# Where the rows of the next block are kept while they wait to be normalised

## The chip, the cores and the metric

The kernel runs on one core of a Trainium2 chip. The metric is the device time of one execution in microseconds (us). The kernel before took 2994.34 us as the median of three runs.

## What is computed

One step of a one-layer encoder, for a prompt of 2048 rows and a sample of 64 rows, all in float32. Cut to what matters here:

```python
mod = jax.nn.silu(c) @ p['w_ada'] + p['b_ada']
sh1, sc1, gt1, sh2, sc2, gt2 = [m[:, None, :] for m in jnp.split(mod, 6, axis=-1)]
h = rms_norm(x, p['norm1_g']) * (1 + sc1) + sh1
z = h @ p['w_in']
glu_a, glu_b, q, k, v, g_conv, g_attn = jnp.split(z, offs, axis=-1)
u = glu_a * jax.nn.sigmoid(glu_b)
# conv module on u; band attention (the own chunk and 8 before it) on the normalised q, k and v
merged = jax.nn.sigmoid(g_conv) * conv_out + jax.nn.sigmoid(g_attn) * attn_out
x = x + gt1 * (merged @ p['w_o'])
# then a second norm with sh2 and sc2, a SwiGLU, and the residual with gt2
```

The modulation `mod` is needed in two parts. The first norm needs `sh1` and `sc1`; the other four vectors (`gt1`, `sh2`, `sc2`, `gt2`) are needed much later.

## The kernel before

A product of two float32 matrices is made of three products of parts (`mm3`): each operand is split into a high part and a low part (`whi` and `wlo`, `hh` and `hl`), so TensorE does three matmuls where one would stand.

The first phase, some 1200 us, goes through the rows in four blocks (`PBLOCKS`): the sample's 64 rows with 512 of the prompt, then three blocks of 512. Within a block the stages come in the order of `ORDER`: the q projection, the first GLU column group (stage 0), k, group 1, v, groups 2 and 3, and the gates `g`. Attention of a block, its convolution and its k/q norms run beside these products as generators in lanes; a planner (`Stream`) decides by estimated engine loads when each lane makes its next step, and what was registered with `stream.at` happens when its planned time comes. The framework's own scheduler then sets the order of the instructions on each engine and allots the buffers of each tag, so a change of what waits for which buffer can move instructions of all engines.

While a block's gates are computed, the rows of the next block are prepared. Each of the four row tiles (128 rows of 1024) goes through `norm_tile`: the row is loaded (`load_x`, a tile called `x_t`), ScalarE squares it (`junk`), VectorE and GpSimd make the inverse root (`ssq`, `t`, then `r` by a power on GpSimd), VectorE scales the row, TensorE turns it in two halves (`pt`), VectorE applies `A1` and `B1` (`h`), ScalarE and VectorE split the result into `hh` and `hl`. The lane `norm_lane` holds two of these generators at a time. The loads are driven by `load_ahead`, which takes the next row from `to_load`: three calls are made at gate `NORM_G` (the eleventh), and one more each time a row's second half has been turned. The rows' buffers have the tag `x`, of which there are three, so the fourth row's load waits until the first row has been turned. The same tag holds `vst` of `store_v` and, in the first block, some of the `kn` tiles of `qk_rows`.

The class `Slabs` (the object `M`) brings the slabs of `w_ada` for the modulation, 512 KB each, into four buffers with the tag `wmod`, in the order of `mod_order`: 16 slabs for `sh1` and `sc1`, used in the first block (keys of five parts), then 32 for the other four vectors, four to each of eight steps (keys of another length). A step is made at the end of each of the GLU stages 0 to 3 of blocks two and three (`MODS`). A slab's load is issued as soon as one of the four buffers is free, whoever will use it and when. So four of the later slabs are loaded in the first block, as the last of the first 16 slabs are used up, and lie in their buffers until the first step of block two; after block three the buffers are not used again.

Weights come through `Weights` (`W`), with five split slabs held; for blocks two to four they are read back as parts that were stored in memory (`w_din_h`, `w_din_l`, `w_dqkv_h`, `w_dqkv_l`). Nearly all loads and stores are issued on SyncE's queue (SP) in one order.

The helper that records every instruction is line 102, so nearly all instructions have that line and are told apart by their tiles; the profile shortens some names (`q2` is `q`, `h32` is `h`).

Of the kernel before, what the change touches and what calls it, by code (L numbers as in the profile page):

```python
# [16 lines left out]
P = 128  # L17
# [15 lines left out]
QB = 512  # L33

PBLOCKS = [(0, 576), (576, 1088), (1088, 1600), (1600, 2112)]
# [11 lines left out]
X_LAG = 8000.0  # L47
# [17 lines left out]
def token_tiles(lo, hi):  # L65
    head = [(0, SMP)] if lo == 0 else []
    return head + [(t, P) for t in range(max(lo, SMP), hi, P)]
# [162 lines left out]
class Slabs:  # L230
# [3 lines left out]
    def __init__(self, sync, other, pool, stream, keys, source, held):  # L234
        self.sync, self.other, self.pool, self.stream = sync, other, pool, stream
        self.keys, self.source, self.held = keys, source, held
        self.ready, self.used, self.given, self.freed = [], 0, 0, 0

    def fill(self):
        while len(self.ready) < min(len(self.keys), self.freed + self.held):  # L240
            (src,), a, b = self.source(self.keys[len(self.ready)])
            w = self.pool.tile([P, a, b], F32, tag="wmod", name="wmod", bufs=self.held)
            i = len(self.ready)
            (self.other if i < self.held and i % 2 else self.sync).dma_start(w, src)
            self.ready.append(w)

    def get(self, key):
        assert self.keys[self.used] == key
        self.used += 1
        while len(self.ready) < self.used:  # L250
            self.free(self.freed + 1)
        return self.ready[self.used - 1]

    def done(self):
        self.given += 1
        self.stream.at(self.stream.when("pe"), lambda n=self.given: self.free(n), True)
# [321 lines left out]
def mod_order():  # L578
    for ct in range(0, KT, 2):
        yield from (("mod", c6, ct // 2, h, 0) for c6 in (0, 1) for h in range(2))  # L580
    yield from (("mod", *half, i) for half in MOD_HALVES for i in range(4))
# [30 lines left out]
def streaming_layer(ctx: ExitStack, tc: tile.TileContext, I, O):  # L612
    nc = tc.nc
    stream = Stream()
    pe, dve, act, gps = (
        Meter(e, n, stream) for e, n in ((nc.tensor, "pe"), (nc.vector, "dve"), (nc.scalar, "act"), (nc.gpsimd, "pool"))
    )
# [10 lines left out]
    def rows(prompt, sample, t, n):  # L628
        return prompt[t - SMP : t - SMP + n] if t >= SMP else sample[t : t + n]
# [129 lines left out]
    def temp(name, shape=(P, 512)):  # L759
        return wk.tile(list(shape), F32, tag="t", name=name, bufs=NT)  # L760
# [353 lines left out]
    def load_x(t, n, pool, tag, bufs, queue=nc.sync):  # L1114
        x_t = pool.tile([P, D], F32, tag=tag, name="x_t", bufs=bufs)
        queue.dma_start(x_t[:n], rows(x_p, x_s, t, n))
        return x_t

    def square(x_t, n):
        ssq = wk.tile([P, 2], F32, tag="ssq", name="ssq", bufs=3)  # L1120
        for j in range(2):
            act.activation(temp("junk")[:n], x_t[:n, 512 * j : 512 * j + 512], AF.Square, accum_out=ssq[:n, j : j + 1])
        stream.after("dve", "act")
        dve.tensor_tensor(ssq[:n, 0:1], ssq[:n, 0:1], ssq[:n, 1:2], ALU.add)
        return rsqrt_mean(wk, ssq[:n, 0:1], n, 1, D)

    ahead_x, to_load = {}, []

    def load_ahead():

        if to_load:
            t = to_load.pop(0)
            ahead_x[t] = load_x(t, P, wa, "x", 3), stream.load["pe"] + X_LAG

    def norm_tile(lo, t, free):

        c = slice(t - lo, t - lo + P)
        while t not in ahead_x:
            load_ahead()
        x_t, landed = ahead_x.pop(t)  # L1140
        yield landed
        r = square(x_t, P)
        yield stream.when("pool")
        dve.tensor_scalar(x_t, x_t, r, None, ALU.mult)
        yield stream.when("dve") + PE_LAG
        for g in range(2):
            pt = ps_g.tile([P, 4, P], F32, tag="gp", name="pt")
            h = temp("h32", (P, 4, P))
            for k in range(4):
                pe.transpose(pt[:, k], x_t[:, (4 * g + k) * P : (4 * g + k + 1) * P], ident)  # L1150
            if g:
                stream.at(stream.when("pe"), load_ahead, True)
            stream.after("dve", "pe")
            for k in range(4):
                kk = 4 * g + k
                dve.tensor_scalar(h[:, k], pt[:, k], A1[:, kk, 0:1], B1[:, kk, 0:1], ALU.mult, ALU.add)
            yield stream.when("dve")
            yield lambda: free["columns"] >= c.stop
            f = slice(4 * g, 4 * g + 4)
            act.activation(hh[:, f, c], h, AF.Copy)  # L1160
            yield stream.when("act")
            dve.tensor_tensor(hl[:, f, c], h, hh[:, f, c].bitcast(F32), ALU.subtract)
    def qkv(b, m, norms):
        lo, hi = PBLOCKS[b]
        tiles = token_tiles(lo, hi)
        ws = {}

        def product(t, n, ps, k):
            if k // 2 not in ws:
                ws[k // 2] = W.get(("qkv", m, k // 2))  # L1170
            wh, wl = ws[k // 2]
            c = slice(t - lo, t - lo + n)
            mm3(ps[:n], hh[:, k, c], hl[:, k, c], wh[:, k % 2], wl[:, k % 2], k == 0, k == KT - 1)
            if (t, n) == tiles[-1] and k % 2:
                W.done()

        for t, n in tiles:
            if t in norms:
                norm_lane.drain([norms[t]])
            ps = ps_g.tile([P, 512], F32, tag="gp", name="ps")  # L1180
            for k in range(KT):
                product(t, n, ps, k)
            if m == 0:
                work.start(qk_rows(ps, n, gqk[:, 0:1], q_d, t, None))
            elif m == 1:
                work.start(qk_rows(ps, n, gqk[:, 1:2], k_d, kcol(t), state_row(ks_p, kn_s, t, n), b == 0 and t > 2 * P))
            else:
                v_rows(ps, n, t)
# [391 lines left out]
    wa = side.enter_context(tc.tile_pool(name="wa", bufs=1, side="right"))  # L1580
    vectors_ = load_vectors()
    first_vectors = next(vectors_)
    M = Slabs(nc.sync, nc.scalar, wa, stream, list(mod_order()), source, 4)
# [8 lines left out]
    for b, stage in ORDER:  # L1592
        lo, hi = PBLOCKS[b]
        if stage == "q":
            free, ahead = {"columns": 0}, {}
            if b + 1 < len(PBLOCKS):
                ahead = {t: norm_tile(hi, t, free) for t, _ in token_tiles(*PBLOCKS[b + 1])}
        if stage == "q" and b == 0:
            pass
        elif stage in ("q", "k", "v"):  # L1600
            qkv(b, "qkv".index(stage), norms)
            if stage == "k":
                work.wide = 3
            if stage == "v":

                def heads(b=b):
                    work.drain()
                    stream.flush()
                    attention(b)
                    if b == 3:  # L1610
                        attn.burst, attn.spacing = 2, 0.0

                stream.at(stream.load["pe"] + HEADS_NS, heads)
        elif stage == "g":
            for g in gates(b, free):
                if g == NORM_G:
                    to_load += list(ahead)
                    for _ in range(3):
                        load_ahead()
                    for gen in ahead.values():  # L1620
                        norm_lane.add(gen)
                if g == SIDE_G and b == len(PBLOCKS) - 1:
                    work.drain()
                    conv.drain()
                    stream.flush()
                    side.close()
                    wc = ctx.enter_context(tc.tile_pool(name="wc", bufs=1, side="right"))
                    cs = tile_chunks(*CBLOCKS[0])[0]
                    src = load_mixed(*cs, 0)
                    first_gates = gate_columns(*cs, 0)  # L1630
            norms = ahead
        else:
            if b == 0 and stage == 1:
                bias_rows()
            if stage == 0:
                conv.drain()
                tail.drain()
                y = wk.tile([P, 4, YW], F32, tag="y", name="y")
            conv.add(convolve(glu(b, stage), y, stage, b))
            if stage == 3:  # L1640
                if b == 0:
                    tail.add(conv_norm(y, 0, SMP, 0))
                    tail.add(conv_norm(y, SMP + HIST, QB, SMP))
                else:
                    tail.add(conv_norm(y, 0, QB, lo))
        for _ in range(MODS.get((b, stage), 0)):
            next(mods)
# [604 lines left out]
```

## Time and profile before

| | |
|---|---|
| median of the runs | 2994.34 us (2992.63 to 2995.2) |
| the profiled execution, its own time | 2994.99 us |
| its span, first to last instruction | 2993.2 us |
| mean granted clock of TensorE | 0.995 |
| loads of rows in the first phase | 17 (14 of the prompt on SP, 2 on ScalarE's queue, 1 of the sample) |
| loads of slabs of `w_ada` | 48 (46 on SP, 2 on ScalarE's queue) |

The page of the profile gives busy time by engine (PE is TensorE, PEld its weight loads, DVE is VectorE, ACT is ScalarE, POOL is GpSimd, SP is SyncE). Idle time of an engine stands in brackets in front of the instruction that ended it, with the instruction that released it. In a list of windows each row has the window, its length, the busy time of each engine with the number of instructions, then the granted clock of TensorE, the mean busy share of the DMA engines and GB/s.

### The profile page before, as it was taken

The page shows a single profiled execution, that of the slowest core. Times are in us where ns is not written, and L with a number is a line of the kernel's source. Part 1 is how long each engine was busy: PE and PEld are TensorE (multiplying, and loading weights), DVE is VectorE, ACT ScalarE, POOL GpSimd, SP SyncE. Part 2 cuts the span into 40 slices and gives each one's busy share as a digit, 9 for nine tenths or more (in the row PEclk, how much of TensorE's full clock was granted, in tenths as well). Part 3 has the DMA queues.
Part 4 walks back from the last instruction along what each step waited for, and adds up shares of the span by engine and source line. Part 5 has one row for each costly group of instructions (what it writes and reads, how often), then busy time and mean ns, then how long its engine had stood idle before and what let it go on. Part 6 is the DMA issues. An engine that isn't in the chain of part 4 may idle for free.

```text
span 2993.2 us, 44914 instructions
## 1 busy us (share of the span) xinstructions
PE 2912.7 (97%) x16259; PEld 2593.7 (87%) x16259; DVE 2024.7 (68%) x3596; ACT 1355.1 (45%) x2437; POOL 1141.4 (38%) x734
## 2 busy tenths in 40 slices
PE   7999899999999999989999999999999999999999
PEld 4899777787888788888989889999999999999998
DVE  5887687767857885477677755666666657466666
ACT  3335643662456257464444335534444345344442
POOL 0201310111011102354566433256666741466667
PEclk9999999999999999999999999999999999999999
DMA  8889889888987789885444786423333975333333
GB/s 290 289 284 304 266 288 314 282 255 275 308 280 221 275 246 286 254 293 166 141 141 152 232 269 216 138 89 115 118 101 115 307 248 183 96 93 116 116 102 127
DMA packets 467724, 628.06 MB, mean 210 GB/s; under 512 B 36276, under 2 KB 314664, under 8 KB 467501
## 3 DMA queue, kind: packets, MB, share of 16 engines
q1 hardware_dynamic: 453456, 605.58, 62.5%
q10 hardware_dynamic: 14045, 19.60, 1.9%
q8 instruction: 128, 2.10, 0.3%
q14 instruction: 95, 0.78, 0.1%
HBM read 476.53 MB, written 148.54 MB: 209 GB/s over the span
## 4 chain that ended last, share of the span: by engine, by line
PE 80%; DVE 8%; DMA 4%; ACT 2%; POOL 2%; issue 2%; SPq 1%; ACTq 0%; DVEq 0%; POOLq 0%
PE ps L102 51%; PE pd L102 16%; PE pw L102 5%; DVE y L102 3%; PE sc L102 2%; PE po L102 2%; PE ptp L102 2%; DVE wlo L102 1%; PE pt L102 1%; PE pa L102 1%; ACT whi L102 1%; DMA tg<-g_d 1%; POOL r L102 1%; POOL wlo L102 1%; DVE pw L102 1%
## 5 line engine op out<-in xcount | busy, mean ns | idle before, releaser
L102 PE MATMUL ps<-t,whi 128*128 128x384 f32 (+1 forms) x2112 | 502.5, 322 | 8.8 <-ACT t L102 5.0
L102 POOL TENSOR_TENSOR wlo<-wst,whi 128x1024 fp32r<-128x1024 f32 (+1 forms) x157 | 358.4, 2292 | 287.1 <-ACT whi L102 251.6
L102 ACT ACTIVATE whi<-wst 128x1024 fp32r<-128x1024 f32 (+1 forms) x264 | 257.5, 978 | 331.9 <-PE ps L102 113.8
L102 PE MATMUL ps<-b,whi 128*128 128x384 f32 (+1 forms) x1584 | 381.3, 326 | 6.1 <-DVE early L102 3.3
L102 PEld LDWEIGHTS ps<-t,whi 128*128 128x128 f32 x2112 | 367.7, 188 | 15.8 <-ACT t L102 5.2
L102 DVE SCALAR_TENSOR_TENSOR y<-u,wd,y 128x512 f32<-128x512 f32 (+1 forms) x480 | 369.1, 773 | 6.8
L102 PE MATMUL ps<-hh,whi 128*128 128x512 f32 (+2 forms) x992 | 361.5, 364 | 0.0
L102 DVE TENSOR_TENSOR acc<-acc,pd 128x512 f32<-128x512 f32 (+1 forms) x464 | 311.6, 685 | 66.9 <-PE pd L102 64.1
L102 PE MATMUL ps<-hl,whi 128*128 128x512 f32 (+2 forms) x992 | 345.3, 348 | 0.0
L102 PE MATMUL ps<-hh,wlo 128*128 128x512 f32 (+2 forms) x992 | 345.1, 348 | 0.0
L102 PE MATMUL ps<-t,wlo 128*128 128x384 f32 (+1 forms) x1056 | 339.2, 321 | 0.7 <-POOL wlo L102 0.7
L102 PE MATMUL pd<-whi,hid 128*128 128x512 f32 (+1 forms) x1016 | 325.2, 391 | 0.5 <-DVE acc L102 0.5
L102 PEld LDWEIGHTS ps<-b,whi 128*128 128x128 f32 x1584 | 278.6, 189 | 12.0 <-DVE early L102 4.2
L102 POOL TENSOR_TENSOR r<-t,mhalf 128x1 f32<-128x1 f32 (+3 forms) x68 | 84.1, 1239 | 453.2 <-DVE t L102 448.0
L102 PE MATMUL ps<-b,wlo 128*128 128x384 f32 (+1 forms) x792 | 256.9, 325 | 0.0
L102 ACT ACTIVATE pr<-pr,sm 128x640 f32<-128x640 f32 (+3 forms) x272 | 200.3, 747 | 102.8 <-DVE sm L102 100.5
L102 PEld LDWEIGHTS pd<-whi,hid 128*128 128x128 f32 (+1 forms) x1016 | 185.9, 183 | 45.2 <-DVE acc L102 0.9
L102 PEld LDWEIGHTS ps<-hh,wlo 128*128 128x128 f32 x992 | 186.6, 188 | 21.8
L102 PEld LDWEIGHTS ps<-hh,whi 128*128 128x128 f32 x992 | 187.2, 189 | 18.5 <-issue 1.6
L102 PEld LDWEIGHTS ps<-hl,whi 128*128 128x128 f32 x992 | 187.3, 189 | 15.4 <-issue 1.4
L102 PEld LDWEIGHTS ps<-t,wlo 128*128 128x128 f32 x1056 | 198.2, 188 | 1.9 <-POOL wlo L102 1.3
L102 PE MATMUL pd<-wlo,hid 128*128 128x512 f32 (+1 forms) x508 | 198.5, 391 | 0.0
(225 smaller groups left out, 6173.5 us busy)
## 6 DMA issues: line engine op xcount, KB each, us to landing
whi<-w_din_h SPq DMA_DIRECT2D x72, 512.0 KB, 6.7
wlo<-w_din_l SPq DMA_DIRECT2D x72, 512.0 KB, 7.5
wst<-sum_d SPq DMA_DIRECT2D x132, 256.0 KB, 2.7
wfo<-in_w_ffn_out SPq DMA_DIRECT2D x64, 512.0 KB, 3.3
wmod<-in_w_ada SPq DMA_DIRECT2D x46, 512.0 KB, 7.3
sum_d<-ws SPq DMA_DIRECT2D x88, 256.0 KB, 2.9
wst<-in_w_ffn_in SPq DMA_DIRECT2D x84, 256.0 KB, 3.1
wst<-in_w_in SPq DMA_DIRECT2D x40, 512.0 KB, 9.4
```

The source lines that it names most:

```text
L102: self.last = f(*args, **kw)
```

## The change

Rows of blocks two and four are loaded into buffers of the tag `wmod` (four) instead of `x` (three); rows of block three stay in `x`. At the gates of blocks one and three four loads are made ahead instead of three. `Slabs` gets a limit, `open`: at first only the 16 slabs of the first 16 keys may be loaded. The limit is lifted by `open_all`, which also issues the loads that are then due; it is registered, in place of a further `load_ahead`, where the second half of a block's last row tile is turned. So the first four of the 32 later slabs are loaded behind the last row of block two. In blocks three and four `open_all` finds nothing to do.

```diff
@@ class Slabs
         self.ready, self.used, self.given, self.freed = [], 0, 0, 0
+        self.open = sum(len(key) == 5 for key in keys)
+
     def fill(self):
-        while len(self.ready) < min(len(self.keys), self.freed + self.held):
+        while len(self.ready) < min(self.open, self.freed + self.held):
...
+    def open_all(self):
+        if self.open < len(self.keys):
+            self.open = len(self.keys)
+            self.fill()
@@ load_ahead
             t = to_load.pop(0)
-            ahead_x[t] = load_x(t, P, wa, "x", 3), stream.load["pe"] + X_LAG
+            place = ("x", 3) if PBLOCKS[2][0] <= t < PBLOCKS[2][1] else ("wmod", 4)
+            ahead_x[t] = load_x(t, P, wa, *place), stream.load["pe"] + X_LAG
@@ norm_tile
             if g:
-                stream.at(stream.when("pe"), load_ahead, True)
+                stream.at(stream.when("pe"), M.open_all if t + P == lo + QB else load_ahead, True)
@@ the gates of a block
                 if g == NORM_G:
                     to_load += list(ahead)
-                    for _ in range(3):
+                    for _ in range(3 if b == 1 else 4):
                         load_ahead()
```

## The prediction

> **What bounds the kernel now.** I read the page first, then the idle time of TensorE instruction by instruction in the timeline, then windows of granted clock round the idle places, then the timelines of VectorE (DVE), ScalarE (ACT), GpSimd (POOL) and SyncE (SP) in those places.
>
> ```profile
> span 2993.2 us, 44914 instructions
> PE 2912.7 (97%) x16259; PEld 2593.7 (87%) x16259; DVE 2024.7 (68%) x3596; ACT 1355.1 (45%) x2437; POOL 1141.4 (38%) x734
> ```
>
> TensorE is busy for 97% of the span. So what this change is worth is idle TensorE time, or time at half clock, taken out or put in; all other engines have room on average. The profiled execution took 2994.99 us, 1.79 over its span and 0.65 over the median of the runs shown; sums below are made against 2994.99.
>
> The largest gap of TensorE where rows are loaded lies between blocks one and two (starts in us, durations; the bracket is the idle time before, and who ended it):
>
> ```profile
> 344.83 0.66 PE L102 MATMUL pt<-ident,x_t 128*128 128x128 f32 x4 [1.22 <-DVE x_t L102]
> ...
> 356.80 1.09 PE L102 MATMUL pt<-ident,x_t 128*128 128x128 f32 x4 [5.66 <-DVE x_t L102]
> ...
> 374.22 0.40 PE L102 MATMUL ps<-wlo,hh 128*128 128x512 f32 x1
> 374.46 0.39 PE L102 MATMUL ps<-whi,hl 128*128 128x512 f32 x1
> ...
> 374.86 0.44 PE L102 MATMUL ps<-hh,whi 128*128 128x512 f32 x1
> ```
>
> At 344.83 the third row tile of block two is turned, at 356.80 the fourth; at 374.86 block two's first GLU product begins (stage 0). A product is issued every 0.24 us (374.22 to 374.46). The 5.66 us come from the fourth load:
>
> ```profile
> 342.98 1.25 SPq L1116 DMA_DIRECT2D x_t<-in_x_prompt  x1
> ```
> ```profile
> 336.48 0.64 ACT L102 ACTIVATE junk<-x_t 128x512 f32<-128x512 f32 x1
> ...
> 353.33 0.61 ACT L102 ACTIVATE junk<-x_t 128x512 f32<-128x512 f32 x1
> ```
> ```profile
> 354.69 0.16 DVE L102 TENSOR_TENSOR ssq<-ssq 128x1 f32<-128x1 f32 x1 [2.14 <-ACT junk L102]
> ...
> 355.90 0.76 DVE L102 TENSOR_SCALAR x_t<-x_t,r 128x1024 f32<-128x1024 f32 x1 [0.23 <-POOL r L102]
> ```
>
> It is issued at 342.98, since its buffer is free only when the first row is turned; its squares stand on ScalarE behind a head's softmax steps, at 353.33; VectorE can scale the row at 355.90. Where block three's rows are turned, TensorE is busy throughout:
>
> ```profile
> 600.00:650.00 50.00, 50.00 (x322) 44.88 (x321) 34.60 (x87) 33.23 (x69) 3.87 (x5) 1.00 0.90 283
> ```
>
> The clock follows such gaps. Windows of 3.41 us (span, busy time of each engine, granted clock, DMA share, GB/s):
>
> ```profile
> 185.50:188.91 3.41, 1.73 (x9) 0.99 (x8) 2.69 (x10) 1.10 (x4) 0.00 (x0) 1.00 0.56 146
> 188.91:192.32 3.41, 2.94 (x11) 2.73 (x12) 2.61 (x7) 2.22 (x5) 0.00 (x0) 0.50 0.92 288
> ...
> 349.34:352.75 3.41, 1.70 (x8) 0.82 (x6) 1.42 (x6) 2.33 (x6) 0.00 (x0) 1.00 1.03 343
> 352.75:356.16 3.41, 0.00 (x0) 0.00 (x0) 1.25 (x6) 3.36 (x10) 0.56 (x1) 0.50 1.08 389
> 356.16:359.58 3.42, 2.66 (x8) 1.95 (x9) 3.42 (x9) 1.18 (x2) 1.08 (x1) 0.50 1.07 256
> 359.58:362.99 3.41, 3.41 (x9) 2.64 (x8) 3.41 (x11) 3.34 (x6) 1.54 (x1) 0.50 0.44 117
> ...
> 421.01:424.42 3.41, 1.67 (x8) 1.01 (x6) 1.59 (x4) 0.00 (x0) 1.64 (x1) 1.00 1.00 333
> 424.42:427.84 3.42, 2.76 (x13) 2.31 (x14) 3.32 (x12) 1.85 (x6) 0.00 (x0) 1.00 0.99 332
> ```
>
> A window in which TensorE was busy for about half (1.73, 1.70) was followed by one or more at clock 0.50; at 421.01 (1.67) it was not. So half busy is the border. The 5.66 us gap cost besides: 2.66 + 3.41 us of work at half rate, 3.0 us lost.
>
> **The change, part by part.**
>
> *Removed: the late fourth row, -8.7 us.* In block two all four rows go into slab buffers, idle since the first block. Their loads now stand far ahead in SP's queue, three of them in the first block, and the fourth row's squares stand on ScalarE right behind the third's (336.48). The 5.66 us and the 3.0 us go; nothing of the old wait is left.
>
> *Late next in the same place, +6.7 us.* The scheduler orders anew from here to the end of block two's GLU products, and that order, as the changed program's instructions stand engine by engine, is what I price. The fourth row's scaling now stands on VectorE ahead of the score steps of the running head, and so do a row reduction, the k/q norm and the third row's turn:
>
> ```
> DVE: x_t(3) ssq o_s t x_t(4) reduce t8 | pr 128 | kn h h h h | pr 256 | y hl ln | pr 384 | h x8 | pr 512
> PE:  sc128 ps*3 turn(3) ps*3 sc256 ps*6 sc384 turn(3) ps*3 turn(4) ps sc512
> ```
>
> Each score matmul (sc) must wait for the step on VectorE (pr) that empties the one before it, as this row of before shows, 425.08 against a step at 424.74:
>
> ```profile
> 424.74 0.28 DVE L102 CUSTOM_DVE_ANT_0 pr<-sc,bias 128x128 f32<-128x128 f32 x1
> ...
> 424.95 0.74 DVE L102 SCALAR_TENSOR_TENSOR y<-u,wd,y 128x512 f32<-128x512 f32 x1
> ```
> ```profile
> 419.54 0.33 PE L102 MATMUL sc<-kk,q 128*128 128x128 f32 x2
> ...
> 425.08 0.50 PE L102 MATMUL sc<-kk,q 128*128 128x256 f32 x2 [2.40 <-DVE sm L102]
> ```
>
> The durations for the sum:
>
> ```profile
> 344.02 0.75 DVE L102 TENSOR_SCALAR x_t<-x_t,r 128x1024 f32<-128x1024 f32 x1 [4.91 <-POOL r L102]
> 344.69 0.28 DVE L102 CUSTOM_DVE_ANT_0 pr<-sc,bias 128x128 f32<-128x128 f32 x1
> ...
> 346.45 0.42 DVE L102 CUSTOM_DVE_ANT_0 pr<-sc,bias 128x256 f32<-128x256 f32 x1 [0.75 <-PE sc L102]
> ...
> 347.59 0.56 DVE L102 CUSTOM_DVE_ANT_0 pr<-sc,bias 128x384 f32<-128x384 f32 x1 [0.70 <-PE sc L102]
> ...
> 349.88 0.69 DVE L102 CUSTOM_DVE_ANT_0 pr<-sc,bias 128x512 f32<-128x512 f32 x1 [0.79 <-PE sc L102]
> ...
> 357.21 0.68 DVE L102 TENSOR_REDUCE ssq<-sq 128x8 f32<-128x512 f32 x1
> ...
> 359.53 2.63 DVE L102 TENSOR_SCALAR h<-pt,A,B 128x128 f32<-128x128 f32 x8
> ...
> 362.69 0.68 DVE L102 TENSOR_TENSOR kn<-kn,r 128x512 f32<-128x512 f32 x1
> ```
> ```profile
> 358.50 2.62 POOL L102 TENSOR_TENSOR r<-t,mhalf 128x8 f32<-128x8 f32 x1 [2.64 <-DVE t L102]
> ...
> 373.69 1.86 POOL L102 TENSOR_TENSOR r<-t,mhalf 128x8 f32<-128x8 f32 x1 [5.88 <-DVE t L102]
> ```
>
> The third row is scaled from 344.02 as now, done at 344.8. From ssq to the scaling of the fourth took 1.2 us (354.69 to 355.90): it starts at 346.0 and ends at 346.7; the reduction ends at 347.3, pr 128 at 347.7. TensorE, after the turn at 344.83 and three products, stands at 346.0: 1.75 us idle. Then kn waits for GpSimd's 128x8 power, 1.86 to 2.62 us (I take 2.1): 349.5, kn done 350.2, four h at 0.33 each 351.6, pr 256 at 352.1. TensorE has six products (1.4 us) after sc256 and stands at 349.6: 2.6 us idle. At sc512 0.25, before the last row's halves 0.4: 5.0 us in all, against nothing if the actual order of arrivals is kinder, 7 if the power takes 2.62 us and the clock falls. 349.5 to 352.1 empties most of a window: I add one at half clock, 1.7 us.
>
> *The next head's scores, +5.1 us.* In before they stand among products, without a gap. In the new order all five (128, 256, 384, 512 wide and the sample's) stand directly behind one another, after block two's first 24 products. Each waits for its predecessor's pr: 0.42, 0.56 and 0.69 us with the accumulator's read and the hand-over, some 2.1 us for three waits. The first pr stands behind a k/q norm with a 1.86 us power, and comes some 1.5 us after its sc: 3.6 us idle, one window's half clock on top (1.5). Bounds: 1 us, if the norm is early and these waits hide a later one, to 7.
>
> *The head after it, +2.4 us.* Its four later scores, too, stand together, one conv step (0.74) between two pr's: four waits of 0.8 us, 3.25, where before has the 2.40 above; +0.85, and a window's half clock, 1.5. Bounds -2.4 to +5.
>
> *The four slabs, 0 us.* Their loads leave the first block and are issued when the last row is turned, by M.open_all. On SP they stand behind the next head's bias and keys and ahead of the weights of block two's second GLU product:
>
> ```profile
> wmod<-in_w_ada SPq DMA_DIRECT2D x46, 512.0 KB, 7.3
> ```
> ```profile
> whi<-w_din_h SPq DMA_DIRECT2D x72, 512.0 KB, 6.7
> ```
> ```profile
> 368.70 0.33 SPq L466 DMA_DIRECT2D whi<-w_din_h  x1
> ```
> ```profile
> 381.20 0.47 PE L102 MATMUL ps<-hh,whi 128*128 128x512 f32 x1
> ```
>
> 2.1 MB at 389 to 256 GB/s (352.75 and 356.16 above) is 5.4 to 8.2 us of all DMA. Issued at 368.7, the weights come at 375.4 as a median, with the slabs ahead at 381 to 384; they were used at 381.20, and would be at 381.2 - 2.0 + 3.6 = 382.8. That just holds: 0, at worst +2 here and as much at the k weights queued behind. The slabs themselves are used after that. For the first block without them I count 0 (nothing there was priced as waiting behind them; at best -1). The fourth load of block four moves forward with its order on TensorE unchanged: 0.
>
> Sum: -8.7 + 6.7 + 5.1 + 2.4 = +5.5, so 3000.5 us, some 3000 against the median.
>
> **Rivals.**
> - *The clock holds.* By the 421.01 row alone the three new half-busy places cost no clock: +5.5 - 1.7 - 1.5 - 1.5 = +0.8, 2995.8. The Trainium skill, "TensorE: Matmul & The Clock Gate", section "Why this matters for your kernels", says that drops are avoided as long as no idle gap is over about 3 us; by it none of my gaps (2.6 at most) would count. The rows at 185.50 and 188.91 speak against it: a drop without any gap of that length, and so I give it less than half.
> - *The stall simply goes, faster.* If rows and norms come early enough that the scores' waits fall on idle VectorE, only about 1 us is left at each of three places: -8.7 + 2 or so, 2988. For it: VectorE is 68% busy on average. Against: its new order, and the power on GpSimd in the middle. It decides at sc384: idle there under 1 us.
> - *The slabs delay weights.* TensorE waits for w_din or for the k weights, 5 us on top of the sum: 3005. For it: DMA is at a share of 0.99 or more in five of the eight windows round the gaps. It decides at the first product on w_din of column 0.
> - *It does nothing:* the fourth row is late by another wait of the same length, 2995.
>
> **How the numbers follow.** A difference of 0.2% (6 us) is about what a measurement of this kernel can tell from no change. The forecast (clock lost at two or three places): 0.40, of which 0.28 lies over 6 us and 0.12 under. Clock holds: 0.20, within. Stall goes: 0.18, faster. Slabs: 0.20, slower. Nothing: 0.02. So faster 0.18, same 0.34, slower 0.48. The range takes the faster rival's 2988 with a little below it, and the slabs' 3005 with some clock: 2986 to 3007.
>
> **What would show it.** Right: no gap before the fourth row's turn; idle TensorE before sc256 and sc384 near 346 and 350 us, ended by VectorE's sm; then a run of four such waits some 6 us into block two's GLU, and windows at 0.50 there. Wrong: these gaps under 1 us each, or clock 1.00 throughout 340 to 440 us, or a DMA of w_din as the releaser of a product.

## The result and the profile after

| | before | changed |
|---|---|---|
| median of the runs | 2994.77 us (2991.51 to 3000.14, 8 runs) | 3003.05 us (3001.81 to 3006.27, 8 runs) |
| the profiled execution, its own time | 2994.99 us | 3003.67 us |
| its span | 2993.2 us | 3001.8 us |

The changed kernel takes 1.0026 times the time before, 95% interval 1.0018 to 1.0035: 8.3 us more. The forecast was 3000 us in a range of 2986 to 3007.

The head of the page of the changed kernel:

```profile
span 3001.8 us, 44903 instructions
PE 2918.3 (97%) x16259; PEld 2595.1 (86%) x16259; DVE 2026.6 (68%) x3596; ACT 1354.1 (45%) x2437; POOL 1139.8 (38%) x734
```

The work is the same; the time was added in a few places. To find them I set matmuls that stand in the same order in both kernels side by side: just ahead of the third row's turn (before 338.95, changed 340.56) the changed kernel is 1.6 us late, and at the first long wait of block two's attention, in the timelines of TensorE, 9.3 us:

```profile
484.49 0.85 PE L102 MATMUL sc<-kk,q 128*128 128x320 f32 x4 [0.93 <-DVE sm L102]
```
```profile
493.81 0.86 PE L102 MATMUL sc<-kk,q 128*128 128x320 f32 x4 [0.93 <-DVE sm L102]
```

From there to the end it stays near this. So the stretch from 340 to 493 holds most of it. First the place of the late fourth row, changed kernel, TensorE and then VectorE:

```profile
346.45 0.66 PE L102 MATMUL pt<-ident,x_t 128*128 128x128 f32 x4 [1.23 <-DVE x_t L102]
349.20 0.50 PE L102 MATMUL sc<-kk,q 128*128 128x256 f32 x2 [1.40 <-DVE sm L102]
353.05 0.61 PE L102 MATMUL sc<-kk,q 128*128 128x384 f32 x2 [1.96 <-DVE sm L102]
353.51 0.66 PE L102 MATMUL pt<-ident,x_t 128*128 128x128 f32 x4
355.25 1.05 PE L102 MATMUL pt<-ident,x_t 128*128 128x128 f32 x4
```
```profile
347.31 0.76 DVE L102 TENSOR_SCALAR x_t<-x_t,r 128x1024 f32<-128x1024 f32 x1 [0.67 <-POOL r L102]
347.98 0.68 DVE L102 TENSOR_REDUCE ssq<-sq 128x8 f32<-128x512 f32 x1
...
348.85 0.29 DVE L102 CUSTOM_DVE_ANT_0 pr<-sc,bias 128x128 f32<-128x128 f32 x1
...
350.63 0.69 DVE L102 TENSOR_TENSOR kn<-kn,r 128x512 f32<-128x512 f32 x1 [1.48 <-POOL r L102]
...
352.58 0.41 DVE L102 CUSTOM_DVE_ANT_0 pr<-sc,bias 128x256 f32<-128x256 f32 x1
```

The fourth row (the turn at 355.25) has no bracket: nobody waits for it. In its place stand two waits for score steps, 1.40 and 1.96 us, since VectorE does the fourth row and a reduction ahead of the first pr, and kn and four h ahead of the second.

Then the next head, in TensorE's timeline. Its five scores stand together at 378.67 to 383.75, and some 20 us later the turns of its softmax's result (`ptp`) and the products behind them wait for the parts that VectorE makes of it (`pl` is the low one):

```profile
378.67 0.42 PE L102 MATMUL sc<-kk,q 128*128 128x128 f32 x2
379.92 0.50 PE L102 MATMUL sc<-kk,q 128*128 128x256 f32 x2 [0.83 <-DVE sm L102]
380.94 0.62 PE L102 MATMUL sc<-kk,q 128*128 128x384 f32 x2 [0.53 <-DVE sm L102]
382.23 0.73 PE L102 MATMUL sc<-kk,q 128*128 128x512 f32 x2 [0.66 <-DVE sm L102]
383.75 0.51 PE L102 MATMUL sc<-kk 128*64 128x320 f32 x2 [0.79 <-DVE sm L102]
...
403.92 0.55 PE L102 MATMUL ptp<-ident,pr 128*128 128x128 f32 x3 [0.42 <-DVE part_l L102]
...
405.80 0.33 PE L102 MATMUL ptp<-ident,pr 128*128 128x128 f32 x1 [0.65 <-DVE pl L102]
407.40 0.49 PE L102 MATMUL ps<-whi,hh 128*128 128x512 f32 x1 [1.26 <-DVE pl L102]
407.73 0.50 PE L102 MATMUL ps<-wlo,hh 128*128 128x512 f32 x1
```

And the head after it:

```profile
432.26 0.50 PE L102 MATMUL sc<-kk,q 128*128 128x256 f32 x2 [0.34 <-DVE sm L102]
433.29 0.62 PE L102 MATMUL sc<-kk,q 128*128 128x384 f32 x2 [0.53 <-DVE sm L102]
434.57 0.73 PE L102 MATMUL sc<-kk,q 128*128 128x512 f32 x2 [0.66 <-DVE sm L102]
436.09 0.80 PE L102 MATMUL sc<-kk 128*64 128x320 f32 x2 [0.79 <-DVE sm L102]
```

The granted clock in windows of 3.41 us (the column after POOL's): three of the four places are followed by one window at half clock, the next head's scores (381.21) are not.

```profile
350.56:353.97 3.41, 1.45 (x10) 0.98 (x8) 3.34 (x10) 2.23 (x5) 0.04 (x1) 0.99 1.10 356
353.97:357.39 3.42, 3.42 (x13) 2.76 (x12) 3.42 (x12) 1.93 (x4) 0.00 (x0) 0.51 0.34 138
...
381.21:384.62 3.41, 1.96 (x8) 0.85 (x7) 1.74 (x7) 2.61 (x9) 0.00 (x0) 1.00 1.03 420
384.62:388.03 3.41, 3.41 (x23) 2.34 (x23) 1.18 (x7) 3.30 (x9) 0.00 (x0) 1.00 1.00 410
405.09:408.50 3.41, 1.50 (x6) 1.00 (x6) 3.38 (x7) 0.70 (x2) 0.00 (x0) 1.00 1.05 293
408.50:411.92 3.42, 3.42 (x9) 2.62 (x8) 2.13 (x6) 1.40 (x4) 0.62 (x1) 0.50 0.62 214
432.49:435.90 3.41, 1.62 (x6) 0.67 (x5) 3.32 (x10) 2.67 (x9) 0.00 (x0) 0.99 1.02 338
435.90:439.31 3.41, 3.22 (x13) 2.89 (x14) 3.26 (x11) 3.08 (x7) 0.00 (x0) 0.51 1.01 341
```

Last the first block, which no longer loads the four slabs. The same turn of keys stands at 115.01 before and at 110.80 in the changed kernel, 4.2 us earlier. But 2.8 us of these stand already at 57 us, when the kernel before has yet to issue the loads of the four slabs (57.61), so at most the rest can come from them. And at the first head of attention TensorE now waits for keys (before, the same score stands at 185.60 without a wait):

```profile
57.61 4.71 SPq L244 DMA_DIRECT2D wmod<-in_w_ada  x4
```
```profile
115.01 0.43 PE L102 MATMUL pt<-ident,kn 64*128 64x64 f32 x4 [2.26 <-DVE kn L102]
...
185.60 0.34 PE L102 MATMUL sc<-kk,q 128*128 128x128 f32 x2
```
```profile
110.80 0.43 PE L102 MATMUL pt<-ident,kn 64*128 64x64 f32 x4 [1.50 <-DVE kn L102]
...
186.05 0.41 PE L102 MATMUL sc<-kk,q 128*128 128x128 f32 x2 [3.13 <-DMA kk<-k_d]
```

On SP these keys stand behind the stores of v, for which the queue waits 10.0 us for VectorE (the last of three in this row is issued at 167.50), and behind nine transfers of weights:

```profile
156.55 11.27 SPq L1035 DMA_DIRECT2D v_d<-vst  x3
...
178.56 3.87 SPq L1393 DMA_DIRECT2D kk<-k_d  x3
```

VectorE was busy for 21.03 of the 22 us from 128 to 150 before, so it could not follow TensorE: its steps on these tiles of v start from 147.7 to 169.7 us in the changed kernel, from 147.5 to 169.4 before. The lead is given back there. At 300 us the two kernels are level again (a score that starts at 299.02 before starts at 299.12). So the first block costs 0.1 us in this profile, and 1.5 of the 1.6 us at 340 come between 304 and 328 us: the turn of a row waits 1.42 us instead of 1.07, and a product (`po`) 0.83 us for ScalarE where before there was no wait.

### The profile page after: what moved, and what is told of

It reads as the page before. It is cut to its first block, busy times and chain, and to the rows that moved or that the text cites. A ratio compares the mean times of both kernels' runs of the same rounds, so it can differ in the third digit from the quotient of the medians.

```text
span 3001.8 us, 44903 instructions
## 1 busy us (share of the span) xinstructions
PE 2918.3 (97%) x16259; PEld 2595.1 (86%) x16259; DVE 2026.6 (68%) x3596; ACT 1354.1 (45%) x2437; POOL 1139.8 (38%) x734
## 4 chain that ended last, share of the span: by engine, by line
PE 77%; DVE 10%; DMA 5%; ACT 2%; POOL 2%; issue 2%; SPq 1%; ACTq 0%; POOLq 0%; DVEq 0%
PE ps L102 48%; PE pd L102 15%; PE pw L102 6%; DVE y L102 4%; PE sc L102 2%; PE po L102 2%; PE ptp L102 2%; DVE wlo L102 1%; PE pt L102 1%; ACT whi L102 1%; POOL r L102 1%; PE pa L102 1%; DMA kk<-k_d 1%; DVE pr L102 1%; POOL wlo L102 1%
```

## The experiments

Each was timed in five rounds beside the kernel before, on one chip for each group of four. The kernel before took 2993.46, 2994.03 and 2994.28 us in the three groups, so times can be compared across them to about 1 us. Theory A: the loss comes from the order that the early row brings, above all from scores that stand together. Rival B: the four slabs cost where they now come.

### The two halves of the change

The limit alone (rows of all blocks in tag `x`, three loads ahead):

```diff
-            place = ("x", 3) if PBLOCKS[2][0] <= t < PBLOCKS[2][1] else ("wmod", 4)
+            place = ("x", 3)
...
-                    for _ in range(3 if b == 1 else 4):
+                    for _ in range(3):
```

> Only the limit on the slabs and open_all are kept; all rows go into the three buffers of tag x, with three loads ahead, as before the change. Theory A (the loss comes from the order that the early fourth row brings, above all the scores that stand together): the program's order is that of the kernel before up to the second head in block two's GLU, where two scores now touch, so the gap of 5.7 us at the fourth row is back, no four waits near 380 us, and the time is 2994 to 2998 us, +0 to +3 on the kernel before. Theory B (the late slabs cost: weights, keys or the modulation wait behind 2.1 MB at a full DMA): 3000 us or more, with idle TensorE that a DMA ends after the slabs are issued. In the first block, without the four slabs, TensorE should be some 4 us ahead by 130 us by both.

2999.46 us (1.0018, 1.0009 to 1.0026): a miss of theory A, 6 us up. But not by rival B either: the fourth row's gap is back (5.65 us), no idle time of TensorE over 0.5 us is ended by a DMA from 205 to 600 us, and this kernel is 4.4 us late at 205 us, long before the slabs are issued (2.9 at 400, 5.1 at the end). It comes from the keys:

```profile
189.28 0.66 PE L102 MATMUL sc<-kk,q 128*128 128x128 f32 x2 [4.22 <-DMA kk<-k_d]
```

Three windows at half clock follow where before had one: 2 us early at 160 us, where 4 were expected at 130, and 4.4 us late at 205.

Block four's rows alone:

```diff
-        self.open = sum(len(key) == 5 for key in keys)
+        self.open = len(keys)
...
-            place = ("x", 3) if PBLOCKS[2][0] <= t < PBLOCKS[2][1] else ("wmod", 4)
+            place = ("wmod", 4) if t >= PBLOCKS[3][0] else ("x", 3)
...
-                    for _ in range(3 if b == 1 else 4):
+                    for _ in range(4 if b == 2 else 3):
```

> Only block four's rows go into slab buffers, with four loads ahead; block two's rows and the slabs are as before the change. The order on TensorE is that of the kernel before, so theory A gives 2995 us, within 2 of the kernel before; a theory by which block four's half of the change cost or won something gives at least 3 us either way.

2994.42 us (1.0003, 0.9995 to 1.0012). This half does nothing that stands out of the noise. Block two's rows alone were not tried: four further row buffers have no room beside slabs without a limit.

### The order of the scores

```diff
+                with tc.issue_after(pe.last.ins):
                 for d in range(2):
                     pe.matmul(ps[:n, 0, :w], q2[:, d, t : t + n], kk[:, :w], start=d == 0, stop=d == 1)
```

(the two lines under it are indented) in the changed kernel, pin_scores, and in the kernel before, before_pinned:

> The changed kernel with one more rule: each score matmul of the first block's heads is issued behind the TensorE instruction that was written before it, so that the scheduler can't move scores together. In the order the five scores of the next head stand apart again (3, 23, 8 and 69 matmuls between them), three of the head after it still touch; the fourth row stays early. Theory A: the 8.7 us measured at the next head (waits 3.7, late products behind the softmax 3.3, one window at half clock 1.7) go and part of the head after it, so 3003 - 8.7 - 1 = 2993 us, 2990 to 2996. Theory B (slabs): stays at 3000 to 3004.

> The kernel before the change with the same rule for the scores as in pin_scores and nothing else: the control. Fourth row late as before with its gap of some 5.7 us; scores stood apart already. Theory A: 2995 us, 2992 to 2998. If the rule by itself is worth something, pin_scores must be read against this kernel and not against the kernel before.

pin_scores took 2990.76 us (0.9987, 0.9978 to 0.9996), 12.3 less than the changed kernel; before_pinned 2991.32 (0.9990, 0.9981 to 0.9999), 2.1 less than before and a little under its range. The control moved a little, since the rule also reordered the place of its late row, whose turn waits for 3.09 us there instead of 5.66. Some 10 of the 12 us are the order's. To see whose, the same line with `if h == 6 else nullcontext()` behind it, so for one head:

> The changed kernel; only the scores of the next head (the seventh) are issued behind the TensorE instruction written before them. The order is that of the changed kernel up to this head, whose scores then stand apart (3, 23, 8 and 69 matmuls between them); in the head after it four still touch. Theory A (the touching scores of this one head cost 8.7 us: 3.7 of waits, 3.3 of products behind a late softmax, 1.7 at half clock): 3003 - 8.7 = 2994 us, 2992 to 2997. Theory C (what pin_scores won came from several heads): 2997 to 3002.

2989.58 us (0.9989, 0.9978 to 1.0001): 13.5 us less than the changed kernel, more than the 8.7 expected. The scores stand apart and wait for nothing, and products behind the softmax don't wait either:

```profile
376.39 0.47 PE L102 MATMUL ps<-hh,whi 128*128 128x512 f32 x1 [0.27 <-DMA whi<-w_din_h]
377.62 0.50 PE L102 MATMUL ps<-hh,wlo 128*128 128x512 f32 x1 [0.20 <-DMA wlo<-w_din_l]
382.99 0.33 PE L102 MATMUL sc<-kk,q 128*128 128x128 f32 x2
383.91 0.39 PE L102 MATMUL sc<-kk,q 128*128 128x256 f32 x2
```

Between 368 and 459 us this kernel gains 10.0 us on the changed one (from 2.8 to 12.8 us ahead at the same matmuls). What it is ahead before that lies at places whose order is the same; its profiled execution, 2993.32 us, is 3.7 over its median and loses 2.5 us again behind 900 us, so the 13.5 us of the medians are accounted for only in part. Of the head after it the waits stayed (0.53, 0.66, 0.79), but no window at half clock follows: the window of 3.41 us that holds the last two, laid in step with that at half clock at 350.86, has 1.96 us busy (422.54 to 425.95), where the changed kernel has 1.69 (432.42 to 435.83, half clock from there). A window from 421.00 to 424.40 would have had 1.74, so where the borders fall may well decide this, and that is luck. With that window the 8.7 become 10.4, near the 10.0. The first two rows show the slabs, too: without the wait of the scores, the weights behind them come 0.27 and 0.20 us late. In two kernels further down the k weights queued behind come late too: 0.67 us in pin_first (403.43), 0.94 in all_three (392.56).

pin_first adds to pin_scores a priority for the step that empties a score (the call is indented under the line):

```diff
+        with tc.high_priority():
         dve.tensor_tensor_reduce(
```

> pin_scores, with the VectorE step that empties a score (pr) at high priority for the scheduler. In the order the current head's second score now stands ahead of the third row's turn and nine matmuls more lie before its third; VectorE's order up to the first pr is the same. Theory A (the waits for pr at the fourth row, 1.4 and 2.0 us, and the clock behind them are what is left of the loss there): 1 to 4 us less than pin_scores, 2987 to 2990; if these waits only move to the next instruction, the turn: 2991.

3000.45 us (1.0016, 1.0008 to 1.0024), 9.7 more than pin_scores, a miss. At the fourth row one wait went down as meant (1.96 to 1.04). But the priority drew the first head's scores together, and its products now wait for the softmax:

```profile
186.50 0.66 PE L102 MATMUL sc<-kk,q 128*128 128x128 f32 x2 [3.49 <-DMA kk<-k_d]
...
190.54 1.22 PE L102 MATMUL sc<-kk,q 128*128 128x512 f32 x2 [0.66 <-DVE sm L102]
193.82 0.48 PE L102 MATMUL ptp<-ident,pr 128*128 128x128 f32 x1 [2.06 <-ACT pr L102]
```

In the profiles this head costs 3.4 us more than in pin_scores. Another 7.2 are lost between 340 and 440 us, where near 417 a ptp waits 1.87 us for pr, with a window at half clock behind it. Products that wait for a softmax are the pattern of the changed kernel's next head, brought about in another way.

### Why scores that touch must wait

The scores of the first block's heads lie in turn in the two halves of one tile. two_tiles gives each half a tile of its own, with the pool opened and closed so that the banks suffice:

```diff
-                    sc = ps_a.tile([P, 2, 512], F32, tag="s", name="sc")
-                    now["banks"] = [sc[:, 0:1], sc[:, 1:2]]
+                    now["banks"] = [s_pool("b").tile([P, 1, 512], F32, tag=f"s{k}", name="sc") for k in range(2)]
```

> The changed kernel; the scores of the first block's heads go in turn into two tiles of one bank each instead of into the halves of one tile of two banks. In the order the next head's five scores still stand directly behind one another. Theory A (a score waits for the pr of its predecessor because both lie in one tile): now each waits for the one before the last, so of the waits 3.4 us at the fourth row, 3.7 at the next head and 2.5 at the head after it some 2.5, 2.9 and 2.2 go, and with them one or two windows of clock: 3003 - 7.6 - 1.7 to 3.4 = 2992 to 2994 us. Rival D (VectorE's own pace sets it, so that the wait moves to the sample's score or to the products behind the softmax): 2999 to 3003.

2996.46 us (1.0012, 1.0003 to 1.0021), 6.6 less than the changed kernel: between the expected 9 to 11 and rival D, who had 4 at most. Two windows of half clock are still there, behind 402 and 429 us. The scores still touch, so that rows of two fall together:

```profile
375.98 0.70 PE L102 MATMUL sc<-kk,q 128*128 128x128 f32 x4
377.36 1.09 PE L102 MATMUL sc<-kk,q 128*128 128x384 f32 x4 [0.67 <-DVE sm L102]
378.64 0.50 PE L102 MATMUL sc<-kk 128*64 128x320 f32 x2 [0.19 <-DVE sm L102]
...
400.69 0.33 PE L102 MATMUL ptp<-ident,pr 128*128 128x128 f32 x1 [0.64 <-DVE pl L102]
402.29 0.64 PE L102 MATMUL ps<-whi,hh 128*128 128x512 f32 x1 [1.27 <-DVE pl L102]
```

Of 2.81 us of waits at the next head 0.86 are left. The waits of products near 402 stay as they were, 1.27 us against 1.26: these are not the shared tile's, but VectorE's, whose convolution steps stand between the parts.

### The first head's keys

```diff
+        queue = nc.scalar if x in (0, "s") and h == 0 else nc.sync
         for d in range(2):
-            nc.sync.dma_start(q2[HD * d : HD * d + HD, :, :nq].bitcast(F32), ...
-            nc.sync.dma_start(kk[HD * d : HD * d + HD, :nk].bitcast(F32), ...
+            queue.dma_start(q2[HD * d : HD * d + HD, :, :nq].bitcast(F32), ...
+            queue.dma_start(kk[HD * d : HD * d + HD, :nk].bitcast(F32), ...
```

in slabs_alone, in pin_scores and in the kernel before:

> slabs_alone, with the first head's queries and keys loaded on ScalarE's queue instead of SP's, where they stood behind stores of v and of weights. Theory K (the limit costs time because TensorE comes 4 us earlier to the first head, finds no keys, waits 4.2 us and loses three windows of clock, 5 us): the wait at 185 to 189 goes or is under 1 us, and the time is 2999.5 - 4.2 - 2 to 3.4 = 2992 to 2994 us. Theory B (the slabs cost where they come late, after 380 us): 2998 us or more, with the wait gone.

> pin_scores with the first head's queries and keys on ScalarE's queue. Its profile has 2.9 us of waiting for keys at 187 and two windows at half clock (3.4 us lost at most). Theory K: 2990.8 - 2.9 - 1.7 = 2986 us, 2984 to 2989. Theory B: 2990 to 2992.

> The kernel before with the first head's queries and keys on ScalarE's queue and nothing else: the control for slabs_keys and pin_keys. Theory K: TensorE did not wait for keys there, so 2994 us, 2991 to 2996, and slabs_keys' 2988.2 is the gain of the limit (4 us of less traffic in the first block) once it isn't given back. If it is 2988 to 2990 by itself, the queue is the gain and the limit gives nothing.

slabs_keys took 2988.16 us (0.9982, 0.9973 to 0.9991), 11.3 less than slabs_alone and below the 2992 to 2994 expected; pin_keys 2987.69 (0.9976, 0.9966 to 0.9986), 3.1 less than pin_scores; before_keys 2989.15 (0.9982, 0.9973 to 0.9991), 5.1 less than before, where theory K had expected nothing. So the limit costs 6.0 us where the keys are late and gives 1.0, no more than noise, where they are not. That its cost lies in the keys' wait is shown; that it would be a gain otherwise is not. The profiles speak for a gain all the same: at 285 us slabs_keys, pin_keys and all_three, which have the limit and the keys on ScalarE's queue, are 7.2, 6.9 and 5.5 us ahead of the kernel before, while before_keys is 0.1 late (its second score waits 3.53 us for VectorE at 180.81). So what the limit is worth with the keys in time stays open. So does where before_keys gains: in its profile it is 1 us late at 580 us and gains mostly behind 900 us, about half of it where much the same waits (2.18 us at 1006, 4.99 at 1330; before, 2.01 and 4.98) are followed by fewer windows at half clock. One profile can't tell whether that belongs to the change of the queue.

### All together

all_three has the rule for the next head, the keys on ScalarE's queue and the two tiles, in the changed kernel; before_keys_tiles the last two in the kernel before.

> The changed kernel with the next head's scores issued in their written order, the first head's keys on ScalarE's queue and the two tiles for scores. Theory A with K: pin_keys' 2987.7, less some 2.5 at the fourth row and a window of clock there (1.7), less 1.2 at the head after: 2983 us, 2979 to 2986. If the second tile gives nothing: 2987 to 2989.

> The kernel before with the keys on ScalarE's queue and the two tiles: the control for all_three. The late fourth row is back, 5.7 us and 3 of clock; of the waits at scores 2.4 us near 425 and 2 near 187 go with a window each. So 2994 - 4.4 - 1.7 to 3.4 = 2987 us, 2985 to 2990. The difference to all_three is what the change is worth without the order it brought: 5 to 8 us by theory A, nothing if the early row only moves the wait.

all_three took 2985.57 us (0.9975, 0.9966 to 0.9985), before_keys_tiles 2992.10 (0.9988, 0.9979 to 0.9996; above its range, and 3 above before_keys). Of the control's waits, that near 425 was to go and is still there (2.35 us at 421.68, with a window at half clock), and two turns of a softmax wait 1.19 and 2.10 us for pr at its first heads. The two kernels differ by 6.5 us. This is not the early rows' alone, since all_three has the limit and the rule for one head as well: in the profiles it is 2.9 us ahead of its control at 300 us, 4.4 at 340, 9.1 behind the fourth row and 6.6 at 440. At the fourth row, first all_three, then its control:

```profile
342.50 0.60 PE L102 MATMUL pt<-ident,x_t 128*128 128x128 f32 x4
343.63 0.60 PE L102 MATMUL pt<-ident,x_t 128*128 128x128 f32 x4
345.19 0.73 PE L102 MATMUL sc<-kk,q 128*128 128x512 f32 x2 [0.96 <-DVE sm L102]
```
```profile
354.51 1.09 PE L102 MATMUL pt<-ident,x_t 128*128 128x128 f32 x4 [5.65 <-DVE x_t L102]
```

all_three is the fastest kernel of the case by its median, 9 us under before; pin_keys, 2.1 us behind it, is within the noise.

## Why the prediction was right

The sum was +5.5 us, the medians give +8.3, and the sign and the range held. In part this is luck: of the steps one came out 1.6 us lower, another 1.7 higher, and 1.5 us come from a place that the prediction did not price. By its steps:

| step | predicted | in the profile after |
|---|---|---|
| late fourth row | -8.7 | -8.7: gap and half clock both gone |
| new waits in its place | +6.7 | +5.1: 1.40 + 1.96, one window of half clock 1.7 |
| next head | +5.1 | +6.8: scores 2.81, products 2.33, one window 1.7 |
| head after it | +2.4 | +1.6: 2.32 against 2.40, one window 1.7 |
| slabs, and the first block without them | 0 | +0.1 at 300 us |
| between 304 and 328 us | not priced | +1.5 |

- *The removed stall* went as worked out, and the order that I read from the instructions is the one that ran: VectorE did the fourth row, the reduction, pr 128, kn, h and pr 256 in that order. The two large waits were 1.40 and 1.96 us instead of 1.75 and 2.6, as the power on GpSimd held up kn for 1.48 us and not 1.8 (347.7 to 349.5 in the prediction). The two small ones (0.25 and 0.4) did not come.
- *The next head* was the right place with the wrong parts. The pr came soon (379.56), so the scores lost 2.81 us and not 3.6, and no clock: the windows at 0.50 that were to show there did not. What the step left out is the products behind the softmax, 0.42, 0.65 and 1.26 us, with a window behind them. pin_next_head shows that the whole is this head's order: 10.0 us between 368 and 459, which takes in the window of the head after it.
- *The head after it*: the waits are no longer than the one of before, only the clock is lost, and pin_next_head, with the same waits, does not lose it.
- *The slabs* were put at 0 where they come late, and that is what the trace has: the weight behind them is issued at 369.93 and used first at 384.09, without a wait; where the scores don't wait, in pin_next_head, it costs 0.47 us. "For the first block without them I count 0" came out at 0.1 us by 300 us, but as the difference of two terms that the prediction did not have. TensorE is 3.0 us ahead at 170 us and loses 3.5 at the keys, by a wait of 3.13 us and a second window at half clock. Not all of this lead is the limit's: between 105 and 122 us the six kernels with the limit and the keys on SP gain 1.6 to 1.8 us on the kernel before, but up to there they are 0.5 to 2.8 us ahead, and before_keys_tiles, without the limit, is 3.0 ahead. In slabs_alone the keys cost more, 5.2 us in the profile and 6 us in the medians. How much of the 8.3 us of the medians lies in the first block is therefore not known. This wait was no row of before, but VectorE's 21.03 of 22 us and the place of the keys behind v's stores on SP were there to be read.
- *Between 304 and 328 us* the changed kernel loses 1.5 us, at two waits that pin_next_head doesn't have, though its order is the same up to 372 us and it gains 0.8 us there. So this need not belong to the change.
- The table adds up to 6.4 of the profile's 8.6 us. From 340 to 494 us it has 4.8 of 7.7 us; 0.7 are won back behind. In this stretch there are 16 waits over 0.15 us where before has five. A wait costs more than its bracket shows: the product ahead of it takes 0.39 us to its end, where otherwise the next would start after 0.23, and the product behind it is followed after 0.33 us instead of 0.23 (407.40 to 407.73). That is an estimate of 0.26 us for each, 2.9 for the eleven more. The next head's 6.8 us become 8.6 with its seven waits; the expectations count it so (8.7).
- *Rival, the clock holds*: false; three windows at half clock are there, as many as the sum had, though one stands behind the products near 407 and not behind the next head's scores. The Trainium skill, "TensorE: Matmul & The Clock Gate", section "Why this matters for your kernels", has drops avoided while no idle gap exceeds about 3 us; here gaps of 1.96, 1.26 and 0.79 us at most were each followed by a window at 0.50 or 0.51, so in this kernel it does not hold.
- *Rival, the stall simply goes* (2988): not as it stands, since the scores' waits did not fall on idle VectorE (the one 384 wide waits 1.96 us, where this rival needed under 1). With one head's scores set apart the time comes near it, 2989.58, though the two waits at the fourth row are still there (1.41 and 1.97 us).
- *Rival, slabs delay weights* (3005): false; no product waits over 0.15 us for w_din in the changed kernel.

## What to carry to other kernels

A load that comes earlier changes more than its own wait: the scheduler orders all engines anew, and steps that shared one buffer and stood apart can end up together. Read the new order engine by engine before the change is run, price each place where users of one buffer touch, and look behind them for who needs their results. A lead won upstream is worth only what the next queue lets through: ask which load the faster engine will meet first.

## What the hardware showed

- Half clock goes more by how full a window of 3.41 us was than by the longest gap (stretches at half clock last 3.41, 6.83 or 10.24 us). Windows with TensorE busy for 1.45, 1.50 and 1.62 us (1.69 when laid exactly in step) were followed by half clock, one with 1.96 (381.21) was not; a wait of 2.40 us in before (425.08) cost no window, waits of 0.79 us at most cost one at the changed kernel's head after. Near half it is not settled: 1.67 before did not, 1.73 did. And two windows well over half were followed by half clock too, with no gap over 0.53 us in them: 2.22 us busy in two_tiles (426.38) and 2.57 in pin_keys (416.46). Both hold scores that touch; why they count as so empty is open.
- In this program scores in the two halves of one tile wait for one another; with a tile for each half the waits at the next head fell from 2.81 to 0.86 us. Whether the scheduler or the chip makes the halves wait was not tested.
